# Block products spread over PSUM tiles, per-chunk exponentials with a bias, and norms on ScalarE in a two-layer hybrid decoder

## The chip, the cores and the metric

The kernel runs on one core of a Trainium2 chip. The metric is the device time of one execution in microseconds (us). The core's engines are named as in the profile: PE (TensorE, matrix products; PEld is its loading of weights), DVE (VectorE), ACT (ScalarE), POOL (GpSimd) and SP (SyncE, which here issues DMAs).

## What is computed

A decoder trunk of two layers takes one inference step for 512 prompt tokens and 8 sample tokens, 520 columns in all (two halves of 260), with a model width of 1024, in fp32. Layer 0 has an RG-LRU branch and a Mamba-2 branch. Layer 1, where the change lies, is HGRN2 with 16 heads of 128:

```
x = rmsnorm(h, w)
q, f, v, g = split(x @ w_in_c)              # each 16 heads x 128
gate  = lower_bound + (1 - lower_bound) * sigmoid(f);  k = 1 - gate
S_t   = diag(gate_t) * S_{t-1} + k_t v_t^T  # one 128 x 128 state per head
o_t   = q_t S_t
h     = h + (rmsnorm_per_head(o) * w_norm * silu(g)) @ w_out_c
```

The prompt is computed in chunks. With b the running sum of log gates, a chunk's rows are scaled by exp(b - mid) on one side and by exp(mid - b) on the other, where mid is b at the middle of the chunk. Each sample token has a state of its own.

## The kernel before

**Order of the work.** The code does not issue instructions directly. Every call of an engine is recorded in a plan, and `Plan.order` then arranges all recorded calls by their dependencies, by estimated costs per instruction and by PSUM space. Each engine's queue is issued in the resulting order. So all instructions have line 520 in the profile (the line of the loop that issues them; 515 for the loads of ACT's function tables), and one tells them apart by their tiles. The planner follows dependencies by the exact region of a tile that an instruction touches. The semaphore waits of the finished program are derived from that order, afterwards. `side(shift, rate)` records a group of instructions as work to be fitted in later beside the main stream. `later(spare)` sets an amount that is added to the planned release time of a TensorE instruction of the group when what it waits for ran on another engine.

**Products.** Each fp32 product is made of three matmuls of parts (high weights by high data, high by low, low by high). A weight block arrives by DMA in `wraw`; ACT casts its high part (`whir`) and DVE subtracts to get the low part (`wlor`). A matmul of 128x128 weights by 128x260 data is the common form.

**PSUM.** `mmps(name)` gives a tile of [128, 2, 512] fp32, one of two in turn. `grab(name)` gives one of four small tiles of [128, 512], which the steps of heads and samples use (`A`, `kt`, `vt`, `kv`, `o`, `ot`, `vs`, `os` and others).

**Layer 1.** The heads are worked on in eight pairs, pr = 0 to 7. `pair(pr, "fvqg")` makes the projections f, v, q and g of both heads. For the pairs 1 to 7, f and v are made by `strassen`: a product of four blocks by seven block products p1, p6, p7, p2, p5, p3, p4 instead of eight, twice a pair, with sums of weight blocks and of data blocks prepared ahead. A block product is 4 x 3 = 12 matmuls of 128x260, so that a pair has 14 products or 168 matmuls, seven pairs 1176. Each finished product is copied or added from PSUM into a row of SBUF (`l1a` for f, `l1b` for v); that is called its evacuation below. Products are named `sm` in the profile; n counts those of a pair, 0 to 13. Before the change the products 2m and 2m+1 lie in the two halves of one `mmps` tile, seven tiles a pair.

After f comes `decay` (line 1780 on): for each head of the pair a logarithm of the gate, a scan (b), the difference b - mid on DVE, and two exponentials of 128x512 on ACT into `qe` and `kd`. After the pair's projections come `samples` and, per head, `head` (line 1807 on): `A` = kd^T qe by chunk, `kt` = transposed kd, `kv`, the states, the output `o`, its mean square by chunk (`at__1738` holds the scales; a POOL instruction raises them to the power of -1/2), a multiplication of `o` in PSUM by these scales on DVE, its transposition `ot`, and the multiplication by the gate. The output projection `o0` to `o8` follows in parts, some of them between other pairs' projections.

Of the kernel before, what the change touches and what calls it, by code (L numbers as in the profile page):

```python
# [26 lines left out]
HN = N // 2  # L27
# [3 lines left out]
CH = 128  # L31
# [509 lines left out]
def hybrid_decode_step_kernel(ctx: ExitStack, tc: tile.TileContext, I, O, mode="both"):  # L541
# [28 lines left out]
    def mmps(name):  # L570
        return new("psm", [128, 2, 512], "mm", name, 2)
# [11 lines left out]
    def bc(ap, shape):  # L583
        return ap.to_broadcast(shape)

    def tt(out, a, b, op, eng=dve):
        eng.tensor_tensor(out=out, in0=a, in1=b, op=op)
# [1015 lines left out]
    def c4v(ap):  # L1603
        return ap.rearrange("p (c t) -> p c t", c=NCH)
# [6 lines left out]
    def layer1_fast():  # L1611
# [92 lines left out]

        def strassen(pr, names):

            ps, n = None, 0

            def product(u, x):
                nonlocal ps, n  # L1710
                if n % 2 == 0:
                    ps = mmps(f"sm{pr}_{n // 2}")
                out = ps[:, n % 2, :HN]
                n += 1
                hw, lw = u
                for k in range(4):
                    with block(True):
                        for i, (w, b) in enumerate(((hw, x[0]), (hw, x[1]), (lw, x[0]))):
                            pe.matmul(out, lhsT=w[:, k], rhs=b[:, k], start=(k == 0 and i == 0), stop=(k == 3 and i == 2))
                    plans[-1].pos += 0.334  # L1720
                return out

            def steps(nm):
                e, e1 = 2 * pr, 2 * pr + 1
                start, done = (start_f, done_f) if nm == "f" else (start_v, done_v)
                o0, o1 = start(e), start(e1)
                l0, r0, l1, r1 = o0[:, :HN], o0[:, HN:], o1[:, :HN], o1[:, HN:]
                g = units[sec[f"{nm}{pr}"]][0]
                if g not in raw_of:
                    load_group(g)  # L1730
                v = raw_of[g]
                a11, a12, a21, a22 = v[:, :4, :128], v[:, 4:, :128], v[:, :4, 128:], v[:, 4:, 128:]
                s2, s3 = (new("cst", [128, N], "sgt", f"{nm}{pr}s{i}", 2)[:, :512].rearrange("p (k c) -> p k c", k=4)
                          for i in range(2))
                w = split_half(a11)
                with side(-SPLIT_AHEAD):
                    tt(s3, a11, a21, ADD)
                    tt(a21, a21, a22, ADD)
                    tt(s2, a21, a11, ADD)
                p1 = product(w, x11)  # L1740
                copy(l0, p1)
                p6 = product(split_half(s2), u2)
                tt(r0, l0, p6, ADD)
                p7 = product(split_half(s3), t3)
                tt(l1, p7, r0, SUB)
                w = split_half(a12)
                with side(-SPLIT_AHEAD):
                    tt(a12, a12, s2, ADD)
                p2 = product(w, x21)
                tt(l0, l0, p2, ADD)  # L1750
                p5 = product(split_half(a21), u1)
                tt(r1, l1, p5, SUB)
                tt(r0, r0, p5, ADD)
                p3 = product(split_half(a12), x22)
                tt(r0, r0, p3, ADD)
                done(e)
                p4 = product(split_half(a22), u4)
                tt(l1, l1, p4, ADD)
                done(e1)

            for nm in names:
                steps(nm)
# [19 lines left out]
        def decay(hd):  # L1782

            with plans[-1].together(H[hd]["t"], H[hd + 1]["t"]):
                for e in (hd, hd + 1):
                    fn(H[e]["b"][:, :T], H[e]["t"][:, :T], AF.Ln, scale=ch[:, e:e + 1], bias=fb[:, e:e + 1])
            for e in (hd, hd + 1):
                d, p = H[e], e % 2
                b = d["b"][:, :T]
                dve.tensor_tensor_scan(out=b, data0=smask, data1=b, initial=0.0, op0=MUL, op1=ADD)  # L1790
                b4 = c4v(b)
                last, mid = b4[:, :, CH - 1:CH], b4[:, :, CH // 2 - 1:CH // 2]
                kd, qe = A[:, 2080 + p * T:2080 + (p + 1) * T], A[:, 3104 + p * T:3104 + (p + 1) * T]
                w = small[:, p * 4:p * 4 + 4]
                d.update(kd=kd, qe=qe, w=w)
                tt(c4v(kd), b4, bc(mid, [128, NCH, CH]), SUB)
                fn(qe, kd, AF.Exp)
                fn(kd, kd, AF.Exp, scale=-1.0)
                stt(kd, d["t"][:, :T], 1.0, kd, SUB, MUL)
                tt(w.unsqueeze(2), last, mid, SUB)  # L1800
                tt(w[:, :NCH - 1].unsqueeze(2), w[:, :NCH - 1].unsqueeze(2), mid[:, 1:], ADD)
                fn(w, w, AF.Exp)
                ts(w[:, NCH - 1:], w[:, NCH - 1:], cneg[:, e:e + 1], MUL)

        def head(hd):
            d, p = H[hd], hd % 2
            at, kd, qe, w, vt = ats[p], d["kd"], d["qe"], d["w"], d["vt"]
            at4 = c4v(at)

            pa = grab(f"A{hd}")  # L1810
            with block():
                for c in range(NCH):
                    cs = slice(c * CH, (c + 1) * CH)
                    pe.matmul(pa[:, cs], lhsT=kd[:, cs], rhs=qe[:, cs], start=True, stop=True)
            dve.copy_predicated(at4, bc(amask.bitcast(U32).unsqueeze(1), [128, NCH, CH]), c4v(pa))
            pk = grab(f"kt{hd}")
            with block():
                for c in range(NCH):
                    pe.transpose(pk[:, c * CH:(c + 1) * CH], kd[:, c * CH:(c + 1) * CH], ident)
            kt = B[:, 3104 + p * T:3104 + (p + 1) * T]  # L1820
            copy(kt, pk)
            pkv = grab(f"kv{hd}")
            with block():
                for c in range(NCH):
                    cs = slice(c * CH, (c + 1) * CH)
                    pe.matmul(pkv[:, cs], lhsT=kt[:, cs], rhs=vt[:, cs], start=True, stop=True)

            S = E[:, 1024 + p * T:1024 + (p + 1) * T]
            for c in range(NCH):
                cs = slice(c * CH, (c + 1) * CH)  # L1830
                scaled(S[:, cs], pkv[:, cs], w[:, c:c + 1])
            for c in range(1, NCH):
                cs, pv = slice(c * CH, (c + 1) * CH), slice((c - 1) * CH, c * CH)
                stt(S[:, cs], S[:, pv], w[:, c:c + 1], S[:, cs], MUL, ADD)
            sp.dma_start(out=O["c_p"][0, 0, hd], in_=S[:, T - CH:])

            po = grab(f"o{hd}")
            with block():
                for c in range(NCH):
                    cs = slice(c * CH, (c + 1) * CH)  # L1840
                    pe.matmul(po[:, cs], lhsT=at[:, cs], rhs=vt[:, cs], start=True, stop=(c == 0))
                    if c:
                        pe.matmul(po[:, cs], lhsT=qe[:, cs], rhs=S[:, (c - 1) * CH:c * CH], start=False, stop=True)
            ms = small[:, 8 + p * 4:12 + p * 4]
            for c in range(NCH):
                act.activation(kt[:, :CH], po[:, c * CH:(c + 1) * CH], AF.Square, accum_out=ms[:, c:c + 1])
            rsqrt_mean(ms, ms, 128, NCH)
            on = kd
            tt(c4v(on), c4v(po), bc(ms.unsqueeze(2), [128, NCH, 128]), MUL)
            pot = grab(f"ot{hd}")  # L1850
            with block():
                for c in range(NCH):
                    pe.transpose(pot[:, c * CH:(c + 1) * CH], on[:, c * CH:(c + 1) * CH], ident)
            sg, og = d["sg"], d["b"]
            stt(og[:, :T], pot, hcn[:, hd:hd + 1], sg[:, :T], MUL, MUL)
            stt(og[:, T:], d["os"], hcn[:, hd:hd + 1], sg[:, T:], MUL, MUL)
            nonlocal last
            if hd == 14:
                o_ = slot("bc", "ohl2", dt=F32R)
                last = o_[:, :NO], o_[:, NO:]  # L1860
            o, (ah, al) = hd % NO, last or (oh, ol)
            copy(ah[:, o], og)
            tt(al[:, o], og, ah[:, o].bitcast(F32), SUB)
# [66 lines left out]

        for pr in range(8):
            pair(pr, "fvqg")
            with side(SAMPLE_LATE):
                samples(2 * pr)
            for i in range(2):
                with side(HEAD_LATE + i * HEAD_I, HEAD_RATE):
                    head(2 * pr + i)
        last, o_ = None, last
        chunk("o7", 10, 4, add_to_h)
# [315 lines left out]
```

## Time and profile before

| | |
|---|---|
| three runs | 1089.67, 1096.3, 1092.01 us; median 1092.01 |
| the profiled execution | 1095.35 us, of which the span (first to last instruction) 1093.6 |
| granted TensorE clock | 0.992 of full speed on average |
| instructions | 21305 |
| layer 1 up to its last output projection | about 470 to 1040 us of the span |

The page gives the busy time of each engine as a share of the span. A busy TensorE counts from the start of a matmul to its modelled end, so that matmuls overlap in it and short losses between two of them do not show as idle time. The distance from one matmul's start to the next one's shows them. In the chain of waits, PEld and PE waiting for the same thing are two views of one wait, not two to be added.

### The profile page before, as it was taken

Reading aid. Unit: us, or ns where it says so; the run is one execution under the profiler, and the core shown is the slowest. Engines: PE = TensorE matmul, PEld = TensorE weight load, DVE = VectorE, ACT = ScalarE, POOL = GpSimd, SP = SyncE. Lnnn points to the kernel's source line nnn. Section 1 sums busy time; section 2 is a strip of 40 time slices with the busy share of each in tenths; the row PEclk is TensorE's granted clock in tenths of the full one; section 3 lists DMA queues with packets and bytes.
Section 4 is the critical chain, followed back from the end, with each engine's and each line's share of the span. In section 5 each row is a group of like instructions: output and inputs, shape, how many; then the busy total and the mean of one; then the engine's idle time right before and its main releaser. Section 6 shows DMA issues by size and latency. Waiting matters only on the chain.

```text
span 1093.6 us, 21305 instructions
## 1 busy us (share of the span) xinstructions
PE 1037.6 (95%) x8427; PEld 1005.2 (92%) x8427; DVE 852.5 (78%) x1727; ACT 593.4 (54%) x1310; POOL 142.8 (13%) x241
## 2 busy tenths in 40 slices
PE   8999899999999999999998998989999999999995
PEld 8889898899999999999888998989989889899995
DVE  6788788998977556897797877788867789878863
ACT  6588775645563122555474635455455546564553
POOL 4635845100000000010000000001010010100000
PEclk9999899999999999999999999999999999999998
DMA  8612263346693333723424351434432443354311
GB/s 276 235 39 78 79 180 115 117 134 177 211 278 130 116 107 120 239 82 86 144 67 119 119 157 42 119 85 133 123 107 89 104 130 103 103 182 140 103 53 43
DMA packets 129956, 138.44 MB, mean 127 GB/s; under 512 B 13704, under 2 KB 111128, under 8 KB 129832
## 3 DMA queue, kind: packets, MB, share of 16 engines
q1 hardware_dynamic: 129464, 136.64, 40.8%
q8 instruction: 68, 1.11, 0.4%
q10 hardware_dynamic: 160, 0.30, 0.1%
q14 instruction: 40, 0.33, 0.1%
q0 software_dynamic: 224, 0.06, 0.0%
HBM read 111.71 MB, written 25.44 MB: 125 GB/s over the span
## 4 chain that ended last, share of the span: by engine, by line
PE 74%; DVE 9%; DMA 6%; POOL 4%; ACT 4%; issue 2%; SPq 0%; POOLq 0%; ACTq 0%; DVEq 0%
PE sm L520 14%; PE o L520 10%; PE g L520 9%; PE pg L520 8%; PE q L520 6%; PE ob L520 4%; PE z L520 3%; DVE l1a L520 3%; PE xbc L520 2%; PE ag L520 2%; PE ax L520 2%; PE pl L520 2%; POOL csm L520 1%; DVE wlo L520 1%; PE A L520 1%
## 5 line engine op out<-in xcount | busy, mean ns | idle before, releaser
L520 ACT CAST whir<-wraw 128x512 fp32r<-128x512 f32 (+1 forms) x121 | 96.5, 800 | 112.2 <-PE sm L520 43.8
L520 DVE TENSOR_TENSOR wlor<-wraw,whir 128x512 fp32r<-128x512 f32 (+1 forms) x121 | 109.7, 911 | 13.5 <-ACT whir L520 12.2
L520 POOL TENSOR_TENSOR at__1738<-at__1738,nhalf 128x4 f32<-128x4 f32 (+1 forms) x24 | 24.9, 1037 | 496.8 <-DVE at__1738 L520 496.8
L520 PE MATMUL o<-ohl,whir 128*128 128x260 f32 x512 | 84.6, 288 | 1.6 <-DVE l1a L520 1.2
L520 ACT CAST whi<-wraw 128x1024 fp32r<-128x1024 f32 (+1 forms) x56 | 57.7, 1031 | 49.9 <-PE ob L520 34.6
L520 DVE TENSOR_TENSOR wlo<-wraw,whi 128x1024 fp32r<-128x1024 f32 (+1 forms) x64 | 77.3, 1208 | 9.3 <-ACT whi L520 8.8
L520 PEld LDWEIGHTS o<-ohl,whir 128*128 128x128 f32 x512 | 71.2, 191 | 2.9 <-ACT whir L520 1.4
L520 PE MATMUL sm<-uh,whir 128*128 128x260 f32 x224 | 65.6, 293 | 8.3 <-DVE l1b L520 5.7
L520 PE MATMUL sm<-xh,whir 128*128 128x260 f32 x168 | 50.9, 303 | 14.0 <-DVE l1a L520 14.0
L520 PE MATMUL sm<-ul,whir 128*128 128x260 f32 x224 | 63.4, 283 | 0.0
L520 PE MATMUL sm<-uh,wlor 128*128 128x260 f32 x224 | 63.2, 282 | 0.0
L520 PE MATMUL g<-xh,whir 128*128 128x260 f32 x256 | 54.2, 293 | 0.6 <-DVE l1a L520 0.6
L520 PE MATMUL q<-xh,whir 128*128 128x260 f32 x256 | 53.8, 291 | 0.0
L520 PEld LDWEIGHTS sm<-uh,whir 128*128 128x128 f32 x224 | 42.1, 188 | 12.2 <-DVE l1b L520 8.0
L520 PE MATMUL o<-ohl,wlor 128*128 128x260 f32 x256 | 51.9, 284 | 0.0
L520 PE MATMUL q<-xh,wlor 128*128 128x260 f32 x256 | 51.5, 283 | 0.0
L520 PE MATMUL q<-xl,whir 128*128 128x260 f32 x256 | 51.5, 283 | 0.0
L520 PE MATMUL g<-xh,wlor 128*128 128x260 f32 x256 | 51.4, 282 | 0.0
L520 PE MATMUL g<-xl,whir 128*128 128x260 f32 x256 | 51.4, 282 | 0.0
L520 PEld LDWEIGHTS sm<-xh,whir 128*128 128x128 f32 x168 | 31.6, 188 | 20.2 <-DVE l1a L520 19.6
L520 PE MATMUL sm<-xl,whir 128*128 128x260 f32 x168 | 47.5, 283 | 0.0
L520 PE MATMUL sm<-xh,wlor 128*128 128x260 f32 x168 | 47.4, 282 | 0.0
(592 smaller groups left out, 3472.9 us busy)
## 6 DMA issues: line engine op xcount, KB each, us to landing
wraw<-in_c_w_in_dram SPq DMA_DIRECT2D x32, 1024.0 KB
wraw<-in_ab_w_in_dram SPq DMA_DIRECT2D x15, 1024.0 KB
wraw<-in_ab_w_out_dram SPq DMA_DIRECT2D x8, 1024.0 KB
wraw<-in_ple_gate_dram SPq DMA_DIRECT2D x8, 1024.0 KB
wraw<-in_c_w_out_dram SPq DMA_DIRECT2D x8, 1024.0 KB
pl<-pl_d SPq DMA_DIRECT2D x2, 2080.0 KB
smp<-in_state_b_ssm_dram SPq DMA_DIRECT2D x8, 512.0 KB
acy<-acsT_d SPq DMA_DIRECT2D x8, 512.0 KB
```

Source lines behind the costliest of these rows:

```text
L520: getattr(f, name)(*a, **k)
```

## The change

Three things are changed, all in layer 1.

1. In `strassen` the products are placed otherwise. Of each six, the products 0 and 3 share one `mmps` tile, the products 1 and 4 another, and the products 2 and 5 take a small tile each (`sg`). A pair has six `mmps` tiles and four small ones for its 14 products.
2. In `decay` the difference b - mid is no longer formed. DVE forms -mid (128x4), and ACT makes the exponentials by chunk from b itself, with -mid or mid as a bias by partition: eight instructions of 128x128 a head in place of two of 128x512. In `head` the multiplication of `o` by its scales moves from one DVE instruction of 128x512 to four ACT copies of 128x128 with a scale by partition.
3. `samples` and `head` are recorded with `later(0.6)`.

```diff
         def strassen(pr, names):
-            ps, n = None, 0
+            pss, n = [], 0
 
             def product(u, x):
-                nonlocal ps, n
-                if n % 2 == 0:
-                    ps = mmps(f"sm{pr}_{n // 2}")
-                out = ps[:, n % 2, :HN]
+                nonlocal n
+
+                i = n % 6
+                if i % 3 == 2:
+                    out = grab(f"sg{pr}_{n}")[:, :HN]
+                else:
+                    if i < 2:
+                        pss[i:] = [mmps(f"sm{pr}_{n}")]
+                    out = pss[i % 3][:, i // 3, :HN]
                 n += 1
...
                 d.update(kd=kd, qe=qe, w=w)
-                tt(c4v(kd), b4, bc(mid, [128, NCH, CH]), SUB)
-                fn(qe, kd, AF.Exp)
-                fn(kd, kd, AF.Exp, scale=-1.0)
+                nm = small[:, 20 + p * 4:24 + p * 4]
+                ts(nm.unsqueeze(2), mid, -1.0, MUL)
+                for c in range(NCH):
+                    cs = slice(c * CH, (c + 1) * CH)
+                    fn(qe[:, cs], b[:, cs], AF.Exp, bias=nm[:, c:c + 1])
+                    fn(kd[:, cs], b[:, cs], AF.Exp, scale=-1.0, bias=mid[:, c])
...
             on = kd
-            tt(c4v(on), c4v(po), bc(ms.unsqueeze(2), [128, NCH, 128]), MUL)
+            for c in range(NCH):
+                cs = slice(c * CH, (c + 1) * CH)
+                act.activation(on[:, cs], po[:, cs], AF.Copy, scale=ms[:, c:c + 1])
             pot = grab(f"ot{hd}")
...
-            with side(SAMPLE_LATE):
+            with side(SAMPLE_LATE), plans[-1].later(0.6):
                 samples(2 * pr)
             for i in range(2):
-                with side(HEAD_LATE + i * HEAD_I, HEAD_RATE):
+                with side(HEAD_LATE + i * HEAD_I, HEAD_RATE), plans[-1].later(0.6):
                     head(2 * pr + i)
```

**What moves on TensorE.** The first place is the start of pair 1, the first strassen stage. Here is PE's queue before, from the last block of the first product (data `xh`, `xl`) into the second product (data `uh`, `ul`); `sm_0_6140` is the tile that both lie in, and a row's brackets name the engines that it waits for.

```order
L520 MATMUL sm_0_6140<-xl_5506,whir_5532 128x260
L520 MATMUL sm_0_6140<-xh_5494,wlor_5611 128x260
L520 MATMUL sm_0_6140<-uh,whir_5532 128x260
L520 MATMUL sm_0_6140<-ul,whir_5532 128x260
L520 MATMUL sm_0_6140<-uh,wlor_5611 128x260
L520 MATMUL sm_0_6140<-uh,whir_5532 128x260 [waits Activation_49]
L520 MATMUL sm_0_6140<-ul,whir_5532 128x260
```

The second product's first block of three follows the first product directly, and its second block waits for ACT, which evacuates the first product. Here is the same queue after the change, from the last matmuls of the product in `sm_1_6171`, which stands behind the first product (in `sm_0_6139`, ended 13 rows ahead of the wait):

```order
L520 MATMUL sm_1_6171<-uh,whir_5532 128x260
L520 MATMUL sm_1_6171<-ul,whir_5532 128x260
L520 MATMUL sm_1_6171<-uh,wlor_5611 128x260
L520 MATMUL sm_0_6139<-xh_5494,whir_5439 128x260 [waits DVE_49,Activation_49]
L520 MATMUL sm_0_6139<-xl_5506,whir_5439 128x260
L520 MATMUL sm_0_6139<-xh_5494,wlor_5463 128x260
L520 MATMUL sg_2_6196<-uh,whir_5439 128x260 [waits Activation_49]
```

The wait for the evacuation of the first product now stands 13 matmuls behind its end, and the third product follows in a small tile.

**What moves on ScalarE.** The second place is ACT's queue at the decay of the pair 1 (heads 2 and 3). Before:

```order
L515 ACT_TABLE_LOAD
L520 ACTIVATE l1a<-l1a,lbt 128x512 [waits DVE_49]
L520 COPY l1b<-kt_6599 128x512 [waits PE_49]
L520 CAST whir_5439<-wraw_6426 128x512 [waits DMAHW1_49,PE_49]
L515 ACT_TABLE_LOAD
L520 ACTIVATE l1a<-l1a 128x512 [waits DVE_49]
L520 ACTIVATE at__1738<-at__1738 128x4 [waits DVE_49]
```

After (`o_6375` is the PSUM tile of a head's output, so that these four rows are the norm of a head of the pair before):

```order
L520 ACTIVATE l1a<-l1a,lbt 128x512 [waits DVE_49]
L520 CAST whir_5532<-wraw_6234 128x1024 [waits PE_49]
L520 ACTIVATE l1a<-o_6375,at__1738 128x128 [waits Pool_49]
L520 ACTIVATE l1a<-o_6375,at__1738 128x128 x3
L515 ACT_TABLE_LOAD
L520 ACTIVATE l1a<-l1a,at__1738 128x128 [waits DVE_49]
L520 ACTIVATE l1a<-l1a,at__1738 128x128 x3
L520 CAST whir_5439<-wraw_6385 128x1024 [waits DMAHW0_49,PE_49]
```

ACT's exponentials come in pieces of 128x128, the first ones with a bias from `at__1738`, and the norm of a head stands among them, behind POOL.

## The prediction

> **What bounds the kernel now.** The first view is the page's share of busy time, with the chain that ended last.
>
> ```profile
> PE 1037.6 (95%) x8427; PEld 1005.2 (92%) x8427; DVE 852.5 (78%) x1727; ACT 593.4 (54%) x1310; POOL 142.8 (13%) x241
> PE 74%; DVE 9%; DMA 6%; POOL 4%; ACT 4%; issue 2%; SPq 0%; POOLq 0%; ACTq 0%; DVEq 0%
> PE sm L520 14%; PE o L520 10%; PE g L520 9%; PE pg L520 8%; PE q L520 6%; PE ob L520 4%; PE z L520 3%; DVE l1a L520 3%; PE xbc L520 2%; PE ag L520 2%; PE ax L520 2%; PE pl L520 2%; POOL csm L520 1%; DVE wlo L520 1%; PE A L520 1%
> ```
>
> TensorE is the bound, and the largest item on the chain is `sm`, the block products that the change places anew. Their 3% neighbour, `DVE l1a`, holds the evacuations of those products. So a change elsewhere pays only where it shortens a wait of TensorE. The next view sums the seven strassen stages (f and v of the pairs 1 to 7; four of them are shown) with a stage of plain output projection and all of layer 1's middle; the columns are length, busy time of PE, PEld, DVE, ACT and POOL, granted clock, DMA share and GB/s.
>
> ```profile
> 511.80:537.50 25.70, 22.13 (x170) 20.67 (x170) 19.42 (x43) 10.04 (x20) 1.03 (x1) 1.00 0.39 118
> 660.80:687.50 26.70, 23.65 (x188) 22.41 (x187) 20.25 (x38) 16.33 (x31) 1.51 (x1) 1.00 0.19 56
> ...
> 860.20:886.30 26.10, 22.53 (x172) 20.73 (x171) 19.84 (x43) 10.14 (x18) 0.00 (x0) 1.00 0.46 122
> 931.50:959.80 28.30, 26.09 (x210) 24.68 (x209) 23.16 (x49) 17.36 (x42) 3.14 (x3) 1.00 0.40 110
> 992.10:1016.00 23.90, 23.90 (x196) 23.04 (x195) 18.79 (x40) 6.52 (x11) 0.54 (x1) 1.00 0.44 133
> 470.00:1040.00 570.00, 541.69 (x4387) 523.43 (x4387) 457.25 (x1016) 310.74 (x683) 29.45 (x33) 1.00 0.38 112
> ```
>
> At full clock the projection stage issues 196 matmuls in 23.90 us, 0.122 us each, and never idles. The strassen stages, with matmuls of the same shape, lie idle 2.2 to 3.6 us each by these rows, and take more than 0.122 us per matmul: 170 at that pace would be 20.7 us, and the stage takes 25.7. What they wait for stands in the chain of waits of 470 to 1040 us (engine and tile, what released it: us in total, times, longest).
>
> ```profile
> PEld sm L520 <- DVE l1a L520: 19.6, 27, 0.7
> PEld sm L520 <- DVE l1b L520: 8.0, 11, 0.7
> PEld sm L520 <- ACT l1a L520: 4.2, 7, 0.7
> ...
> PEld ot L520 <- DVE l1a L520: 3.1, 3, 1.5
> PE ot L520 <- DVE l1a L520: 2.4, 3, 1.3
> PEld o L520 <- ACT whir L520: 1.4, 1, 1.4
> ```
>
> Forty-five waits of one size, 31.8 us together, all for the engine that evacuates a product. One of them, on the timeline (start, length, engine, operation, and in brackets the idle time ahead):
>
> ```profile
> 517.04 0.29 PE L520 MATMUL sm<-xl,whir 128*128 128x260 f32 x1
> ...
> 517.16 0.28 PE L520 MATMUL sm<-xh,wlor 128*128 128x260 f32 x1
> 517.48 0.43 DVE L520 TENSOR_TENSOR l1a<-sm,l1a 128x260 f32<-128x260 f32 x1 [0.50 <-PE sm L520]
> ...
> 517.97 0.39 PE L520 MATMUL sm<-xh,whir 128*128 128x260 f32 x1 [0.52 <-DVE l1a L520]
> ...
> 518.19 0.29 PE L520 MATMUL sm<-xl,whir 128*128 128x260 f32 x1
> ```
>
> Up to 517.16 matmuls start 0.12 us apart. Then VectorE adds a finished product into `l1a`, and the next matmul, into the other half of the same tile, starts only when that add has ended. In the order of before this follows from the placement: the second product's first block of three stands behind the last block of the first, the evacuation is due between them, and so the second block waits for it although it writes another half. The loss is 517.97 − 517.16 − 0.12 = 0.69 us, and another 0.10 as the next matmul starts 0.22 us later instead of 0.12: 0.79 us a time.
>
> **The change part by part.**
>
> *Placement.* A tile's second product is now the third behind its first. Two products of other tiles, or one of them and a first block, stand between, so at least 13 matmuls: 13 × 0.12 = 1.56 us against the 0.81 us (517.16 to 517.97) that drain, add and restart took. That leaves 0.75 us for VectorE or ScalarE to come late. In the order of before 46 products wait one or two matmuls behind the evacuation's product; after the change three do (in the pairs 1, 3 and 5). Removed: 45 × 0.79 = 35.6 us. Kept: 3 × 0.79 = 2.4 us. New: about 40 waits with a slack of 0.75 us. They cost nothing if the evacuation starts at once; on an engine busy with one instruction of about 0.69 us the slack just covers it.
>
> ```profile
> L520 DVE TENSOR_TENSOR wlor<-wraw,whir 128x1024 fp32r<-128x1024 f32 x49 | 59.8, 1219 | 1.6 <-ACT whir L520 1.1
> L520 DVE TENSOR_TENSOR wlor<-wraw,whir 128x512 fp32r<-128x512 f32 x70 | 47.5, 687 | 11.8 <-ACT whir L520 11.1
> L520 ACT ACTIVATE l1b<-g 128x520 f32<-128x520 f32 x16 | 9.6, 602 | 14.2 <-PE g L520 14.2
> L520 DVE SCALAR_TENSOR_TENSOR l1b<-l1b,g 128x520 f32<-128x520 f32 x16 | 11.1, 695 | 4.2 <-ACT l1b L520 4.0
> ```
>
> VectorE has splits of half a weight block in these stages, 687 ns each. One ahead of the evacuation is covered; two are 2 × 0.687 − 0.75 = 0.62 us too long. I choose one product in eight for that: 5 × 0.62 = 3 us. The ends are 0 (always in time) and, at the 0.79 us of today, 40 × 0.79 = 32 us (always late). I stay near the low end because VectorE has 6 us a stage free, which is worked out again under A.
>
> The second product of a pair (`sm_1`) opens the other tile one product earlier than today, so it needs the `g` projection of the pair before evacuated within 12 × 0.12 = 1.44 us; evacuation is 0.60 on ScalarE and 0.70 on VectorE, 1.30, and its hand-overs. I take 0.2 us for each of seven pairs, 1.5 us; between 0 and 7 × 0.79 = 5.5.
>
> *Exponentials and norms.*
>
> ```profile
> L515 ACT ACT_TABLE_LOAD x24 | 30.8, 1283 | 0.4
> L520 ACT ACTIVATE l1a<-l1a 128x512 f32<-128x512 f32 x32 | 20.2, 630 | 7.1 <-DVE l1a L520 6.9
> L520 ACT ACTIVATE l1c<-l1c,l1d 128x128 f32<-128x128 f32 x64 | 20.0, 392 | 0.0
> L520 ACT ACTIVATE l1d<-kv,at__1738 128x128 f32<-128x128 f32 x51 | 15.8, 366 | 7.9 <-PE kv L520 4.5 <-DVE l1d L520 3.2
> L520 DVE TENSOR_TENSOR l1a<-l1a 128x512 f32<-128x512 f32 x16 | 11.0, 688 | 0.2
> L520 DVE TENSOR_TENSOR l1a<-o,at__1738 128x512 f32<-128x512 f32 x16 | 11.0, 686 | 4.4 <-POOL at__1738 L520 4.4
> L520 DVE TENSOR_SCALAR at__1738<-at__1738 128x4 f32<-128x4 f32 x16 | 2.6, 164 | 6.8 <-ACT l1b L520 6.8
> ```
>
> VectorE loses 11.0 + 11.0 and gains 16 × 0.164 = 2.6 us: −19.4, from 457 to 438. ScalarE loses 20.2 and gains 128 exponentials and 64 scaled copies of 128x128, both with a pointer operand. The nearest rows are 20.0 / 64 and 15.8 / 51, 0.31 us of busy time each, so 40.0 + 19.8; the order has six more table loads, 6 × 1.283 = 7.7. Net +47 us, from 311 to 358 of some 541: 66%. Neither engine sets the pace by its total. By head the decay chain grows from 0.69 + 2 × 0.63 = 1.95 to 0.16 + 8 × 0.31 = 2.64 us and the norm from 0.69 to 1.24. Cover is the projection of q, g or the next f on TensorE. Without cover both would cost 1.24 us × 16 = 20 us. The last head has no next pair; its cover is this:
>
> ```profile
> 986.23 0.69 DVE L520 TENSOR_TENSOR l1a<-o,at__1738 128x512 f32<-128x512 f32 x1 [1.12 <-POOL at__1738 L520]
> ...
> 1003.70 0.74 DVE L520 SCALAR_TENSOR_TENSOR l1a<-ot,hcn,l1b 128x512 f32<-128x512 f32 x1
> ```
>
> From its norm to its gate 17 us pass, of which four transposes and two instructions are work; 0.55 us more vanishes. I count 0, between −3 us (what the waits for `ot` above hold, if later placement ends them) and +8 us.
>
> The Trainium skill, "ScalarE: Activation LUTs", section "Rules for kernel authors", says to give adds and multiplies to VectorE rather than ScalarE; that speaks against the moved norm. The rows agree as to engine time (19.8 us for 11.0), and on a bound ScalarE the sum would be 8.8 us worse; with 34% of it free I leave the sum as it is.
>
> *Later placement of head and sample steps by 0.6 us.* It changes where the planner puts TensorE's small steps, not their number. Counted in the 0 above. SyncE issues the same DMAs, some weight loads ahead of sample loads; no wait of TensorE in the chain of waits is for a DMA.
>
> *Sum.* −35.6 + 2.4 + 3 + 1.5 = −28.7 us. The profiled execution took 1095.35 us around a span of 1093.6 and lies 3.3 us above the median of 1092.01, which is within what the three runs spread (1089.67 to 1096.3); so the median is the base: **1063 us**.
>
> **The rivals.**
>
> A. VectorE takes the place of the wait. In the strassen stages it is busy 19.4 to 20.3 us (23.2 in the last); freed of stalls, TensorE needs 20.7 to 22.9 us. Then VectorE stands at 88 to 94% and evacuations queue behind splits. For it: those two numbers. Against: 19 us less work on it, and the projection stage above at 18.79 of 23.90 us without any stall. Price: half of the removed wait returns, 14 to 15 us: 1078.
>
> B. The waits do not hang on the tile. Then nothing but VectorE's relief remains, 1090 ± 3. The row of 517.97 speaks against it: a wait for an add that reads the other half. The Trainium skill, "PSUM — Partial Sum Buffer", section "PSUM bank collisions raise a hardware error", asks for guards by bank and partition quadrant and reports accesses to different banks as clean. By that rule the two halves, 512 fp32 apart, need no wait, and the placement would be worth nothing. The trace disagrees: the wait is there, whoever asks for it.
>
> C. Slower: the small PSUM tiles. Four one-bank tiles serve all head and sample steps; now 28 block products (four a pair, seven pairs) take one too, and TensorE, in order, stands until ScalarE or VectorE has emptied it. With ScalarE 47 us busier, that could be late. At the longest wait that TensorE shows for a head step, 1.5 us (`PEld ot`), 28 × 1.5 = 42 us: 1063 + 42 = 1105. It decides from 29 / 28 = 1.04 us a tile on. Against: the head steps are spread over pairs, and today TensorE shows four such waits.
>
> **How the numbers follow.** Forecast 0.76, A 0.15, B 0.04, C 0.05. The range of the forecast itself: low, with late evacuations, `sm_1` and the three kept waits at 0 and the heads at −3, −35.6 − 3 gives 1053, and the median before is itself known to a microsecond or two; high, evacuations late by 8 us more and the heads at +6, 1077. Rival A up to its middle and that uncertainty give **1052 to 1079**. About 1% is what a measurement of this kernel can tell from no change, 11 us. A is faster still by 1.3% but its upper half is not; of A 0.09 goes to faster and 0.06 to same, of the forecast 0.74 to faster and 0.02 to same, B to same but for 0.01, C to slower: faster 0.83, same 0.11, slower 0.06.
>
> **What the profile after would show.** Waits of the weight loads of `sm` on `l1a` and `l1b` fall from 31.8 us to under 7; the strassen stages shrink from some 26 us to 21 or 23; PE sits at 97% or more. VectorE in layer 1 shows 19 us less, ScalarE 47 more, with 128x128 exponentials near 0.31 us of busy time. Wrong would be the forecast if `sm` keeps 15 us or more of waits with longer single ones (A), if 45 waits of 0.7 us remain (B), or if waits of `sg` on head tiles appear (C).

## The result and the profile after

| | before | after |
|---|---|---|
| median of the runs | 1092.08 us (4 runs, 1089.67 to 1096.3) | 1055.18 us (4 runs, 1052.58 to 1057.9) |
| profiled execution | 1095.35 us, span 1093.6 | 1052.58 us, span 1050.9 |

The ratio is 0.9658, with a 95% interval of 0.962 to 0.9697: 37 us less, where 29 were forecast, inside the range. The profiled execution of before lies 3.3 us above its median and that of after 2.6 us below its own, so the two traces differ by 42.8 us, six more than the medians. Nearly all of the six lies ahead of everything that was edited: layer 1's first `q` matmul starts at 481.8 us in the one trace and at 476.0 us in the other.

The page of after, busy time and the chain's lines:

```profile
PE 1023.1 (97%) x8427; PEld 1000.0 (95%) x8427; DVE 832.6 (79%) x1705; ACT 630.8 (60%) x1482; POOL 139.4 (13%) x241
PE o L520 10%; PE sm L520 9%; PE q L520 9%; PE pg L520 9%; PE g L520 8%; PE ob L520 4%; PE sg L520 4%; PE xbc L520 2%; PE ax L520 2%; DVE wlo L520 2%; PE oa L520 2%; PE pl L520 2%; PE z L520 1%; DMA smp<-in_state_b_ssm_dram 1%; POOL csm L520 1%
```

The same 8427 matmuls fill 97% of a shorter span. `sm` and `sg` together stand at 13% of the chain, and the evacuations (`DVE l1a`, 3% before) are no longer among its lines. The chain of waits of TensorE's weight loads from 470 us on:

```profile
PEld sm L520 <- DVE l1a L520: 2.2, 3, 0.7
...
PEld g L520 <- DVE l1a L520: 1.3, 1, 1.3
PEld sm L520 <- issue: 1.1, 5, 0.2
...
PEld sm L520 <- DVE l1b L520: 0.6, 2, 0.3
...
PEld sg L520 <- DVE l1d L520: 0.2, 1, 0.2
```

Of the 45 waits of 0.7 us three remain, 2.2 us together; they are the three neighbours in one tile that the forecast kept. The small tiles bring one wait of 0.2 us for another engine. The timeline at the start of the first strassen stage shows a second product that follows in its tile:

```profile
507.44 0.28 PE L520 MATMUL sm<-xh,wlor 128*128 128x260 f32 x1
...
507.56 0.28 PE L520 MATMUL sm<-uh,whir 128*128 128x260 f32 x1
...
507.75 0.43 DVE L520 COPY l1a<-sm 128x260 f32<-128x260 f32 x1
...
508.88 0.28 PE L520 MATMUL sm<-uh,wlor 128*128 128x260 f32 x1
...
509.00 0.28 PE L520 MATMUL sm<-xh,whir 128*128 128x260 f32 x1
```

The first product ends with the matmul of 507.44, and a product of another tile follows at once (507.56 to 508.88). VectorE copies the first one out from 507.75 to 508.18. The matmul that needs this, at 509.00, starts 0.12 us behind its neighbour, 0.8 us after the copy ended: that much of the slack was left over. The next view sums three strassen stages and the layer by windows (columns as in the prediction):

```profile
504.70:530.40 25.70, 25.18 (x206) 24.11 (x205) 23.97 (x60) 15.77 (x44) 2.63 (x3) 1.00 0.52 142
638.30:661.00 22.70, 22.18 (x181) 21.45 (x180) 20.89 (x50) 12.39 (x31) 1.55 (x2) 1.00 0.54 157
827.20:850.60 23.40, 23.29 (x192) 22.57 (x191) 22.22 (x55) 13.44 (x38) 1.59 (x3) 1.00 0.57 155
455.00:1000.00 545.00, 541.14 (x4487) 531.52 (x4486) 448.32 (x1011) 353.43 (x865) 27.67 (x33) 1.00 0.41 120
```

The first strassen stage of before had 170 matmuls in 25.70 us, that of after 206 in the same length, 0.125 us each. So this stage did not shrink to the 21 to 23 us that the forecast named; it took in 36 more matmuls, of other steps. The other two rows, 22.7 and 23.4 us, lie near that. VectorE now stands at 92 to 95% in these stages.

To size it over the layer, the distance from each matmul's start to the next one's was summed by tile over the traces. The 1176 block-product matmuls took 176.2 us before and 148.8 after: −27.4 us. Everything else of layer 1 gave another 9.7 us: `q` −4.5, `os` −1.5, `vs` −1.4, `kv` −0.8, the rest under 0.7 each. A wait is booked here on the matmul ahead of it: of the 4.5 us of `q`, 2.6 are a wait of `ot` and one of `vs` that followed it before.

### The profile page after: what moved, and what is told of

Its sections match the earlier page's. It is cut to its first block, busy times and chain, and to the rows that moved or that the text cites. A ratio compares the mean times of both kernels' runs of the same rounds, so it can differ in the third digit from the quotient of the medians.

```text
span 1050.9 us, 21517 instructions
## 1 busy us (share of the span) xinstructions
PE 1023.1 (97%) x8427; PEld 1000.0 (95%) x8427; DVE 832.6 (79%) x1705; ACT 630.8 (60%) x1482; POOL 139.4 (13%) x241
## 4 chain that ended last, share of the span: by engine, by line
PE 73%; DVE 10%; DMA 6%; ACT 4%; POOL 3%; issue 2%; SPq 0%; POOLq 0%; ACTq 0%; DVEq 0%
PE o L520 10%; PE sm L520 9%; PE q L520 9%; PE pg L520 9%; PE g L520 8%; PE ob L520 4%; PE sg L520 4%; PE xbc L520 2%; PE ax L520 2%; DVE wlo L520 2%; PE oa L520 2%; PE pl L520 2%; PE z L520 1%; DMA smp<-in_state_b_ssm_dram 1%; POOL csm L520 1%
## 5 line engine op out<-in xcount | busy, mean ns | idle before, releaser
L520 POOL TENSOR_TENSOR at__1738<-at__1738,nhalf 128x4 f32<-128x4 f32 (+1 forms) x24 | 22.6, 942 | 461.5 <-DVE at__1738 L520 455.5
L520 DVE TENSOR_TENSOR h<-h,o 128x520 f32<-128x520 f32 x40 | 27.8, 694 | 26.2 <-PE o L520 25.9
L520 PE MATMUL sm<-uh,whir 128*128 128x260 f32 x140 | 40.4, 289 | 1.8 <-DVE l1a L520 1.6
L520 PE MATMUL sm<-xh,whir 128*128 128x260 f32 x140 | 41.4, 296 | 0.0
L520 PEld LDWEIGHTS g<-xh,whir 128*128 128x128 f32 x256 | 39.2, 189 | 2.2 <-DVE l1a L520 1.3
L520 PE MATMUL sm<-xh,wlor 128*128 128x260 f32 x140 | 39.6, 283 | 0.3 <-DVE wlor L520 0.3
L520 PE MATMUL xbc<-xnh,whi 128*128 128x260 f32 x192 | 39.7, 289 | 0.0
L520 PE MATMUL sm<-xl,whir 128*128 128x260 f32 x140 | 39.6, 283 | 0.0
```

What stands on the lines that cost most here:

```text
L520: getattr(f, name)(*a, **k)
```

## The experiments

All ratios are to the kernel before on the same chip, with 95% intervals.

**The placement alone** (the edit of `strassen`, nothing else).

> Only the placement of the block products is changed. Theory: the 45 waits of 0.7 us hang on the tile that two neighbouring products share, so nearly all go: the weight loads of sm wait under 5 us instead of 31.8, and the time falls by 27 us (the measured loss of sm between the two profiles) to about 1065, while about 10 us of waits at head and sample steps stay. Rival 1, VectorE has to be relieved for the evacuations to be in time: half of it, about 1078, with waits of sm above 12 us. Rival 2, order of the whole layer did it: nothing, 1092.

Measured: 1059.43 us against 1094.11, ratio 0.9686 (0.9657 to 0.9716). The weight loads of its trace from 470 us on:

```profile
PEld os L520 <- DVE l1d L520: 3.6, 2, 2.6
...
PEld sm L520 <- DVE l1a L520: 0.7, 1, 0.7
```

One wait of 0.7 us is left. `sm` and `sg` take 146.3 us in place of 176.2, which is −30.0, and the rest of layer 1 −1.7. Rival 1 falls with it: VectorE has as much work here (850.4 us on the page) as before (852.5), and the evacuations are in time all the same, to within 0.3 us.

**The exponentials alone, the norm alone, later placement alone.**

```diff
-                tt(c4v(kd), b4, bc(mid, [128, NCH, CH]), SUB)
...
+                ts(nm.unsqueeze(2), mid, -1.0, MUL)
...
```

> Only the exponentials by chunk with a bias. Theory: 45 waits of 0.7 us at sm remain, VectorE has 8.4 us less and ScalarE 20 more, neither of them the bound: 1092 within 4. Rival, the shorter VectorE queue ends the waits at head steps: 1084 or less.

Measured: 1095.0 us, ratio 1.0013 (0.9994 to 1.0032). As expected; `sm` waits at 28, 13 and 7 places, where before it was 27, 11 and 7.

```diff
-            tt(c4v(on), c4v(po), bc(ms.unsqueeze(2), [128, NCH, 128]), MUL)
+            for c in range(NCH):
...
+                act.activation(on[:, cs], po[:, cs], AF.Copy, scale=ms[:, c:c + 1])
```

> Only the norm's multiplication on ScalarE. Theory: the sm waits remain, VectorE has 11 us less and ScalarE 20 more: 1092 within 4. Rival, the waits of ot for the norm (3.1 us, three times) and those behind them go: 1084 or less. Other rival, a norm of 1.24 us in place of 0.69 makes ot wait longer: 16 x 0.55 = 9 us more, 1101.

Measured: 1104.19 us, ratio 1.0094 (1.0066 to 1.0122), slower by 10 us. Neither story fits: `ot` lost 2.1 us, not 9. The largest single loss in the trace (of the slowest of the six runs) is a wait of a `g` matmul, by the waits of 553 to 562 us:

```profile
DVE f2s L520 <- DMA wraw<-in_c_w_in_dram: 3.5, 1, 3.5
PEld g L520 <- issue: 3.5, 1, 3.5
PE g L520 <- DVE l1a L520: 3.3, 1, 3.3
```

VectorE sat at the sum of weight blocks `f2s`, whose DMA had not landed. The evacuation of `q` (`l1a`, at 559.0) stood behind it in the same queue, and TensorE waited for that. In the order of this kernel the sum stands ahead of the evacuation; the norm itself is nowhere in that chain. The wait also cost more than its length: up to 565.7 us the granted clock was 0.50, and 26 matmuls took 5.7 us where 3.1 would do at 0.12 each. Wait and half clock make some 5.9 of the 9.9 us that layer 1 lost in this trace.

```diff
-            with side(SAMPLE_LATE):
+            with side(SAMPLE_LATE), plans[-1].later(0.6):
...
```

> Only the 0.6 us of later placement for head and sample steps. Theory: this is what ended the waits of TensorE at ot, vs and os, about 10 us in the comparison of the two profiles: 1082, with the sm waits unchanged at 31 us. Rival, the moved steps only wait elsewhere: 1092 within 4.

Measured: 1102.52 us, ratio 1.0065 (1.0038 to 1.0092), slower by 8 us where 10 us of gain were expected. The `os` matmuls did take 1.6 us less, but in the trace a wait of `g` for `l1a` of 3.2 us and one of `sm` for `l1b` of 3.0 us are new. The first has the cause found above: VectorE waited 5.4 us for the DMA of a weight block, and the evacuation of `q` stood behind that sum. The second is an evacuation of `g` behind other work in VectorE's queue. After each the granted clock was 0.50 for 3.4 us.

**All three without the placement.**

> Exponentials, norm and later placement, without the new placement of products. Theory: beside neighbours in one tile the three edits are worth nothing or less, since the waits of TensorE at sm (45 to 49 of 0.7 us) stay: 1095 within 6. Rival, they add up as measured alone (+1, +10, +8): 1113. Other rival, together they save the 10 us that went from head steps in the comparison of the two profiles: 1083.

Measured: 1092.69 us against 1091.88, ratio 1.0004 (0.9988 to 1.002). Three edits that measure +1, +10 and +8 us alone give nothing together. In its trace:

```profile
PEld sm L520 <- DVE l1a L520: 20.4, 28, 0.7
PEld sm L520 <- DVE l1b L520: 10.7, 13, 1.4
PEld sm L520 <- ACT l1a L520: 4.9, 8, 0.7
```

So the stalls stay with the old placement, though VectorE has 15.6 us less work on the page (836.9 against 852.5). The rest of layer 1 takes 6.1 us less than before (`q` −3.1, `os` −1.6), but the block products take 6.0 us more (182.2 against 176.2), and nothing is left of it.

**The whole change without later placement.**

> The whole change without the 0.6 us of later placement. Theory: the placement carries all but a few microseconds, so 1057 to 1062; the order has eight more TensorE steps close behind what they wait for, worth 4 us at most. Rival, later placement is what makes the norm on ScalarE bearable (+10 alone): 1068 or more.

Measured: 1063.91 us, ratio 0.9741 (0.9717 to 0.9764), between the two expectations, and not faster than the placement alone (0.9657 to 0.9716).

**A tile of its own for each product.**

```diff
-                if n % 2 == 0:
-                    ps = mmps(f"sm{pr}_{n // 2}")
-                out = ps[:, n % 2, :HN]
+                ps = mmps(f"sm{pr}_{n}")
+                out = ps[:, 0, :HN]
```

> Only one edit against before: each block product opens a tile of two banks of its own and leaves its other half empty, 14 tiles a pair, no small tiles. Theory, the stall comes from neighbours in one tile: no product then waits one or two matmuls behind the evacuation of its neighbour, 62 wait 13 behind it, and the time falls as with the new placement, to 1060 within 5. Rival, the gain comes from the room of the small tiles, with which evacuations may be two products late: then with two tiles in turn at most half is gained, 1075 or more.

Measured: 1069.0 us, ratio 0.9783 (0.976 to 0.9806), 9 us short of the theory and outside its bounds. But `sm` takes 146.2 us in the trace, as little as with the placement alone. No `sm` wait of 0.7 us remains. The shortfall lies elsewhere, its largest piece in one wait, by the waits of 623.5 to 630 us:

```profile
DVE f3s L520 <- DMA wraw<-in_c_w_in_dram: 6.7, 1, 6.7
...
PE g L520 <- DVE h L520: 4.5, 1, 4.5
```

The window behind it (the last three figures are the granted clock, the DMA share and GB/s):

```profile
629.20:634.90 5.70, 5.66 (x25) 4.93 (x26) 2.36 (x3) 0.01 (x1) 0.00 (x0) 0.50 0.44 96
```

It is the same again: VectorE waited for the DMA of a weight block, the residual addition `h` stood behind that sum, and a `g` matmul behind the addition. In the 5.7 us that followed, the granted clock was 0.50 and 25 matmuls ran, which need 3.0 us at 0.12 each. The wait and the half clock make about 7.2 us of the 8.4 by which layer 1 is longer than with the placement alone. So the stalls come from neighbours in one tile; the room of the small tiles is not needed to end them.

**All products in the small tiles.**

```diff
-                if n % 2 == 0:
-                    ps = mmps(f"sm{pr}_{n // 2}")
-                out = ps[:, n % 2, :HN]
+                out = grab(f"sg{pr}_{n}")[:, :HN]
```

> Only one edit against before: all 14 products of a pair lie in the four small tiles that head and sample steps use too. Theory: neighbours are apart, so the 45 stalls go, but 98 products now share four banks with head steps in order, and each late head step stands ahead of TensorE: 1063 to 1080, with waits of sg for A, kv, o or ot in the chain of waits. Rival C of the prediction, a small tile costs 1 us and more a time: 98 x 1 us, above 1120. Other rival, no cost at all: 1059.

Measured: 1087.84 us, ratio 0.9953 (0.9932 to 0.9973), above the expected range.

```profile
PEld sg L520 <- DVE l1a L520: 13.5, 7, 3.4
PEld sg L520 <- ACT l1a L520: 6.2, 5, 1.6
PEld sg L520 <- ACT l1d L520: 3.6, 3, 1.2
PEld sg L520 <- DVE wlor L520: 2.4, 5, 0.6
```

The neighbours are apart, and yet the products take 175.3 us. The first three rows hold 23.3 us of waits for 98 products, 0.24 us each. But three of the waits in the first row, 3.2 us each by PE's own, are not for a head step. They are for the evacuation of a product (`l1a<-l1a,sg`, at 572.09, 714.05 and 856.52 us), which stood behind a run of small instructions on `l1c` and `l1d` in VectorE's queue. Behind each of the three the granted clock was 0.50 for 3.3 to 5.8 us. So rival C is real in kind, but what a small tile costs by itself is not shown by this run.

**Two subsets with the placement.** First the placement with later placement only.

> The placement and the later placement of head and sample steps, without the exponentials and the norm. Theory: the placement gives 34 us, later placement beside it takes a few waits at os, vs and q away: ratio 0.96 to 0.968, 1048 to 1057. Rival, the relief of VectorE by 19 us is needed for the last part: 0.972 or more.

Measured: 1059.76 us against 1093.31, ratio 0.9695 (0.9671 to 0.9718). Then the whole change without the norm.

> The whole change without the norm on ScalarE. Theory: the norm is worth nothing beside the placement, or costs up to 10 us as alone: ratio 0.957 to 0.966, 1045 to 1055. Rival, the shorter norm work on VectorE carries part of the gain: 0.970 or more.

Measured: 1059.41 us, ratio 0.9688 (0.9666 to 0.971). Both lie just above what was expected and cannot be told from the placement alone (0.9686).

**Other amounts of later placement** (`later(0.6)` replaced by the number, in the whole change).

> The whole change, with 0.3 us of later placement in place of 0.6. Theory: what the three small edits are worth beside the placement is a matter of which few steps the planner puts where; the number shifts it by some us up or down without a trend, sm waits stay under 5 us, ratio between 0.963 and 0.975. Rival, later placement gives slack in proportion: midway between 0.974 without it and 0.966 with 0.6, so 0.970, and better at 0.9 than at 0.6.

> The whole change, with 0.9 us of later placement in place of 0.6. Theory: no trend, between 0.963 and 0.975, with single waits of 1 to 4 us at other places than before. Rival, slack in proportion: 0.962 or less.

| later by | 0 | 0.3 | 0.6 | 0.9 |
|---|---|---|---|---|
| ratio | 0.9741 | 0.9704 | 0.9658 | 0.9778 |
| interval | 0.9717 to 0.9764 | 0.968 to 0.9729 | 0.962 to 0.9697 | 0.9755 to 0.9801 |

At 0.3 the two theories could not be told apart (0.9704 fits both). At 0.9 the kernel is 8 us slower than at 0.3, so slack in proportion is refuted; 0.9778 lies beyond the other theory's bound too. `sm` takes 148.1 to 148.8 us at 0.3, 0.6 and 0.9 alike. In the traces layer 1 is 7.0 us longer at 0.9 than at 0.3, spread over `vs` (2.3), `o` (1.7), `g` (1.1), `os` (1.0) and smaller ones. Some of the waits at 0.9, of which the last stands at 0.3 too:

```profile
PEld o L520 <- DVE h L520: 2.2, 3, 1.1
...
PEld os L520 <- DVE l1d L520: 1.9, 1, 1.9
PEld o L520 <- ACT l1a L520: 1.7, 1, 1.7
```

No version tried is faster than the change as it stands. That 0.6 is the best of four amounts without a trend may be the luck of one order; no run here shows a reason.

## Why the prediction was right, and where it was off

**The mechanism held, and the placement's terms nearly balance.** Forecast at −28.7 us in sum, they measure −27.4 on the block products in the whole change and −30.0 with the placement alone. Term by term the balance is partly luck. The trace of before has 43 starts of a block product that stand over 0.6 us behind the one ahead, 28.9 us beyond the pace of 0.12 in all; after has three, 2.0 us (518.24, 651.08 and 784.49). So stalls gave 26.9 us net, where 33.2 were forecast. The 0.10 us for the restart, 4.5 us of the 35.6, came back in the change: losses of 0.04 to 0.5 us within the products sum to 6.4 us before, 3.6 with the placement alone and 5.8 after, where many stand next to sample steps (`os`, `ot0s` and the like) among the products. On the other side late evacuations of products, put at 3 us, do not show, and the earlier start of the second tile, put at 1.5, costs 0.27 us in each of two pairs.

**Off: the term of head and sample steps.** It was put at 0, between −3 and +8; the traces have −9.7 us there. The waits of `ot` and `vs` that before showed are mostly gone. The cover for the longer chains held. Three of the waits that went were of `ot` for the norm, which is one of the edited instructions. But they go without that edit too: with the placement alone TensorE's matmuls of `ot` wait 0.2 us for it in place of 2.4, `q` takes 3.4 us less and `vs` 1.4, while `os` has a new wait of 2.3. So they hang on where the planner puts a few steps, and a new order has others; which order comes out well was not forecast and is luck here. The runs bound what they are worth: 0 without the placement (1.0004), and beside it 0.9658 against 0.9686, with intervals that overlap. So about 34 of the 37 us are the placement's, and whether the other edits add three is not shown.

**Rival A: its load came, its price did not.** VectorE is busy 23.97 of 25.70 us in the first stage, 93%, as A said, and TensorE keeps its 0.125 us a matmul. Occupancy was the wrong measure here: an evacuation of a product has 0.75 us to spare, and in the trace of after none was late apart from the three kept neighbours. Those of `g` were late twice, by 0.3 us, and one of `q` by 1.1. What stands right ahead of an evacuation in VectorE's queue decided, as the run with all products in small tiles shows.

**Rival B fell** by the placement alone and by the runs without it. The rule of the Trainium skill, "PSUM — Partial Sum Buffer", section "PSUM bank collisions raise a hardware error", that it was weighed with is not contradicted, although the prediction says that the trace disagrees. The waits of before stand in the program, and two other placements remove them. Whether the chip would have needed a wait between halves of one tile was not tried.

**Rival C** stays small: in the change's trace the small tiles cost a wait of 0.2 us, far from 1.04 us each. With 98 of them the waits come to 0.24 us each, late evacuations included.

**ScalarE and VectorE.** Forecast were −19.4 us on VectorE (page: 852.5 to 832.6, −19.9) and +47 on ScalarE (593.4 to 630.8, +37.4). The rows of the new instructions agree with the forecast:

```profile
L515 ACT ACT_TABLE_LOAD x30 | 38.5, 1283 | 0.5
L520 ACT ACTIVATE l1a<-l1a 128x128 f32<-128x128 f32 x64 | 21.4, 391 | 0.1
L520 ACT ACTIVATE l1a<-l1a,at__1738 128x128 f32<-128x128 f32 x64 | 20.5, 390 | 0.4 <-DVE at__1738 L520 0.3
...
L520 ACT ACTIVATE l1a<-o,at__1738 128x128 f32<-128x128 f32 x64 | 18.9, 361 | 5.0 <-POOL at__1738 L520 5.0
```

21.4 + 20.5 − 20.2 + 18.9 + 7.7 = 48.3 us. The eleven that are missing on the page did not go to other engines: the durations of all other ScalarE instructions sum to 612.6 us, against 612.7 before. Records of neighbouring instructions overlap, and the page counts an overlap once.

## What to carry to other kernels

When an in-order engine stalls for the same short time again and again, compare what the wait guards with what the waiting instruction writes. Here two independent products shared a tile, and spacing them by one product ended 42 of 45 stalls without making anything faster. Before adding buffers, look at who else takes them in turn. Look also at what an evacuation stands behind: in three of these runs that was a sum whose weights were still on the way, and TensorE stood for 3.2 to 4.5 us. And where a planner arranges the queues, measure each edit with its companions: alone, an edit may show mostly what the new order happened to put behind a late transfer.

## What was not expected

VectorE at 92 to 95% of a stage, feeding a TensorE that waited for it 0.3 us (22.22 of 23.40 us at 827 us). And, with the norm alone, one late DMA of a weight block cost 3.3 us of TensorE, through an evacuation that stood behind its sum in VectorE's queue; the sum stood at 555.9 us and was first read at 571.5.

The prediction did not reckon with the granted clock. In the runs here each of the seven waits of TensorE in layer 1 of 3.0 us or more (one with the norm alone, two with later placement alone, one with a tile for each product, three with all products in small tiles) has a stretch of 3.4 or 6.8 us at a granted clock of 0.50 around its end or up to 1.0 us behind it, and the 128x260 matmuls there start about 0.215 us apart in place of 0.12. Shorter waits have such a stretch in some places and not in others. The trace of before has one in layer 1, and after has none:

```profile
617.90:621.30 3.40, 3.40 (x18) 3.40 (x17) 2.31 (x4) 0.31 (x2) 0.00 (x0) 0.50 0.42 78
```

It came behind two waits of 1.0 and 1.2 us, and its sixteen matmuls lost 1.5 us. So the price of one long wait is more than its length.
